# Weight block sums of seven-product sets: two of four made by adding DMAs, and the second weight tile in a slot of its own

## The chip, the cores and the metric

The kernel runs on one core of a Trainium2 chip. The metric is the device time of one execution in microseconds, as a median of several runs.

The core has TensorE (PE: matmuls, and PEld its weight loads), VectorE (DVE), ScalarE (ACT), GpSimd (POOL) and SyncE (SP), which issues most of the DMAs. Each engine carries out its own instructions strictly in the order in which they stand in the program, and waits on semaphores for the others.

## The reference

Two layers of a streaming encoder work on 512 tokens of 1024 channels. Each layer has a feed-forward network (FFN), a mixer of three branches, and a second FFN. The change lies in the FFNs alone:

```python
def swiglu(h, w_gate, w_up, w_down):
    return (jax.nn.silu(h @ w_gate) * (h @ w_up)) @ w_down
    ...
    h = modulate(rms_norm(x, norm_gain[l, 0]), mod[:, 0], mod[:, 1])
    x = x + 0.5 * mod[:, 2][:, None, :] * swiglu(h, ffn_w_gate[l, 0], ffn_w_up[l, 0], ffn_w_down[l, 0])
```

The hidden width is 2816, which is 22 blocks of 128 columns. All inputs are float32.

## The kernel before, in words

**Number format.** TensorE multiplies a rounded format (fp32r). To keep float32 accuracy every operand is split in two: a high half, made by a cast on ScalarE, and a low half, the rest, made by a subtraction on VectorE (`split_to`, L416 to L418). A product is then three matmuls: high by high, high by low, low by high.

**An FFN** goes through the 22 blocks in three parts of 6, 8 and 8 blocks. In each part the gate and up products are made, silu of the one is multiplied with the other, and the result goes through w_down (`k_outer`, L421 on), which adds to the residual x. The blocks of the first part are made directly (all six in the very first FFN, four of six in the others). All other blocks are made in pairs.

**A pair of blocks** is made by a seven-product scheme of block matrices (Winograd's form of Strassen's method): `seven`, L541. It is called once for w_gate (a gate set) and once for w_up (an up set). The weights of the two blocks, each 1024 x 128, form a 2 x 2 grid: A11 and A12 are the first and second half of the first block's rows, A21 and A22 those of the second block. The tokens h form a grid B11 to B22 too. Seven products of half size take the place of eight. Their left sides are A11, A12, A22 and the sums S1 = A21 + A22, S2 = S1 - A11, S3 = A11 - A21, S4 = A12 - S2; their right sides are B11, B21, B22 and the sums T1 to T4, which the class `Blocks` makes once per FFN.

A set does the following. SP loads the two weight tiles of 512 KB ("raw", two buffers, L547). The first tile is split, and A22 too. VectorE makes the four sums (L556 to L559) into two tiles of the "v2" slots, one with S1 and S2, one with S3 and S4. Both are split into tiles of the "ptb" slots. These are two buffers, so the split of a set's S1 and S2 waits until the set before has finished its products with S1 and S2. Then come the products, each of 12 matmuls of 256 columns (4 blocks of rows by 3): A11, A12, S2, S1, S3, S4, A22. Between them ScalarE copies partial results out of PSUM into a tile c, and VectorE adds to it (L573, L582, L583). After an up set, VectorE multiplies with the silu of the gate set (`act`, L624) and splits the result.

**How often.** The second and the third part of each of the four FFNs are a run of eight sets (gate and up in turn). The first part of three FFNs has a lone pair of sets. That makes 8 x 8 + 3 x 2 = 70 sets.

**The order of the work.** Python writes the instructions in the order of the code; small pieces of side work (`later`, `poll`) are put between matmuls by due times. The framework then fixes, when the program is built, in what order each engine's instructions stand, and which buffer each tile gets. SP's queue is also in order: a load that waits for its buffer holds up the loads behind it. MOD_RATE is 0 in the runs of sets, so that the loads of w_ada, which feed the modulation, stand in w_down's stages.

Of the kernel before, what the change touches and what calls it, by code (L numbers as in the profile page):

```python
# [40 lines left out]
def encoder_kernel(tc, xT, c, w_ada, b_ada, gains, w_gate, w_up, w_down, w_qkv, w_f, w_ubg,  # L41
# [443 lines left out]
    def minus(o, a, b):  # L485
        nc.vector.tensor_tensor(o, a, b, op=ALU.subtract)  # L486

    class Blocks:
# [28 lines left out]

        def t1_t3(self, m):
            b1, b2 = self.full[m], self.full[m + 2]
            minus(b1[:, :, FIRST], b1[:, :, SECOND], b1[:, :, FIRST])  # L520
            minus(b1[:, :, SECOND], b2[:, :, SECOND], b1[:, :, SECOND])

        def t2_t4(self, m):
            b1, b2 = self.full[m], self.full[m + 2]
            minus(b2[:, :, SECOND], b2[:, :, SECOND], b1[:, :, FIRST])
            minus(b2[:, :, FIRST], b2[:, :, FIRST], b2[:, :, SECOND])

        def split(self, q):
            self.parts[q] = blk("b"), blk("b")
# [10 lines left out]

    def seven(srcs, blocks, bank):  # L541

        raws = []
        for src in srcs:
            side_work()
            raw = st([P, KD, P], F32, "raw", NRAW)
            last["dma"] = nc.sync.dma_start(raw, src).ins  # L547
            raws.append(raw)
        tens = lambda o, a, b, op: nc.vector.tensor_tensor(o, a, b, op=op)
        a11, a12, a21, a22 = raws[0][:, :4], raws[0][:, 4:], raws[1][:, :4], raws[1][:, 4:]  # L550
        ah, al = duo((KD, P), "w", NARROW)
        split_to(ah, al, raws[0])
# [25 lines left out]
        nc.scalar.copy(c[:, 2], w)  # L578
        go(x, "S3", "T3", False)
        nc.scalar.copy(c[:, 3], x)  # L580
# [15 lines left out]
    class Ffn:  # L596
# [19 lines left out]
        def act(self, n, pg, pu, sg=None):  # L616
            if sg is None:
                sg = apply([pg], AF.Silu)
            pr = t2(T)
            parts = pu if isinstance(pu, list) else [pu]  # L620
            m = T // len(parts)
            for i, p in enumerate(parts):
                cols = slice(i * m, (i + 1) * m)
                nc.vector.tensor_tensor(pr[:, cols], p, sg[:, cols], op=ALU.mult)  # L624
            a = blk("b")
            split_to(a[:, 0, :], a[:, 1, :], pr)
            return a

        def run(self, nxt):
# [4 lines left out]
            for part, (f0, nf) in enumerate(parts):  # L634
# [41 lines left out]
                if not opening:  # L676
                    blocks.finish()
                while n < nf:
                    both = [apply(p, AF.Silu)
                            for p in seven([w_gate[l, s, f0 + n + i] for i in range(2)], blocks, acc)]  # L680
                    ups = seven([w_up[l, s, f0 + n + i] for i in range(2)], blocks, mmt)
                    for i, sg in enumerate(both):
                        acts.append(self.act(n + i, None, ups[i], sg))
                    n += 2
                MOD_RATE[0] = 1.2
                for c0 in (0, T):
# [644 lines left out]
```

## Time and profile before

| what | value |
|---|---|
| time, median of 3 runs | 2368.86 us (2366.21 to 2369.56) |
| the profiled execution's own time | 2370.22 us |
| its span in the profile | 2368.4 us |
| granted TensorE clock | 1.00 |
| bytes moved by DMA | 325.18 MB |

The page gives for each engine its busy time and its share of the span. The rows of groups read: line, engine, operation, output and inputs, count, then busy time and the mean of one, then the idle time of the engine ahead of them and what ended it. Busy time of TensorE is modelled for the ends of matmuls, so the starts of rows tell its pace better than their lengths; the same holds for VectorE and ScalarE, where an instruction's end overlaps the start of the next.

### The profile page before, as it was taken

To read this page: it belongs to the slowest core of one execution; us is meant where nothing else is said; L and a number is where in the kernel's file an instruction comes from. 1 tells how busy PE (TensorE), PEld (TensorE's weight loads), DVE (VectorE), ACT (ScalarE), POOL (GpSimd) and SP (SyncE) were. 2 spreads that over 40 slices of the span, in tenths; PEclk is the share of its full clock that TensorE was granted. 3 is DMA by queue.
4 is the path that set the end of the run, shared out by engine and by line. 5 is a ranking of instruction groups with operands and counts; after the bars stand their busy time and mean duration, and the time that the engine had idled before them with its cause. 6 is when DMAs were issued, how large, how long until landed. Compare 5 with 4: busy or idle time off the path is not lost.

```text
span 2368.4 us, 37435 instructions
## 1 busy us (share of the span) xinstructions
PE 2335.2 (99%) x14322; PEld 2075.8 (88%) x14322; DVE 1770.8 (75%) x3147; ACT 1197.2 (51%) x2097; POOL 326.4 (14%) x433
## 2 busy tenths in 40 slices
PE   7999999999999999999999999999999999999999
PEld 5898998878888898989999989888788888999898
DVE  8887866787686577878687878677866855878583
ACT  5353555676632353635553536456765324636262
POOL 3000011244411100000100000112543211000000
PEclk9999999999999999999999999999999999999999
DMA  8535342333355524353415353533333654143233
GB/s 292 182 107 187 101 167 88 105 99 110 122 199 202 188 71 161 116 187 99 152 63 178 101 185 107 187 107 99 99 122 106 221 199 167 63 142 108 98 100 107
DMA packets 117976, 325.18 MB, mean 137 GB/s; under 512 B 11650, under 2 KB 13826, under 8 KB 117796
## 3 DMA queue, kind: packets, MB, share of 16 engines
q1 hardware_dynamic: 115106, 314.38, 39.9%
q0 software_dynamic: 2688, 8.39, 1.2%
q8 instruction: 113, 1.85, 0.3%
q14 instruction: 67, 0.55, 0.1%
q10 hardware_dynamic: 2, 0.00, 0.0%
HBM read 312.16 MB, written 6.38 MB: 134 GB/s over the span
## 4 chain that ended last, share of the span: by engine, by line
PE 85%; DVE 9%; ACT 3%; DMA 2%; issue 2%; SPq 0%; ACTq 0%; DVEq 0%; POOL 0%; POOLq 0%
PE acc L140 16%; PE acc L142 16%; PE acc L141 16%; PE mm L151 4%; PE mm L149 4%; PE mm L150 4%; PE acc L149 4%; PE acc L151 4%; PE acc L150 4%; PE mm L140 3%; PE mm L142 3%; PE mm L141 3%; PE mm L1020 1%; DVE w L418 1%; DVE v L486 1%
## 5 line engine op out<-in xcount | busy, mean ns | idle before, releaser
L312 DVE TENSOR_TENSOR w<-raw,w 128x1024 fp32r<-128x1024 f32 x247 | 313.2, 1271 | 161.6 <-ACT w L310 161.3
L310 ACT CAST w<-raw 128x1024 fp32r<-128x1024 f32 (+1 forms) x255 | 264.3, 1040 | 273.4 <-PE acc L142 187.5
L140 PE MATMUL acc<-b,w 128*128 128x512 f32 (+1 forms) x960 | 359.8, 375 | 0.0
L141 PE MATMUL acc<-b,w 128*128 128x512 f32 (+1 forms) x960 | 356.3, 371 | 0.0
L142 PE MATMUL acc<-b,w 128*128 128x512 f32 (+1 forms) x960 | 356.1, 371 | 0.0
L142 PEld LDWEIGHTS acc<-b,w 128*128 128x128 f32 x960 | 180.4, 188 | 31.6
L140 PEld LDWEIGHTS acc<-b,w 128*128 128x128 f32 x960 | 180.3, 188 | 30.3
L141 PEld LDWEIGHTS acc<-b,w 128*128 128x128 f32 x960 | 180.6, 188 | 29.8
L417 ACT CAST ptb<-v 128x1024 fp32r<-128x1024 f32 x140 | 146.6, 1050 | 100.8 <-DVE v L486 62.0
L418 DVE TENSOR_TENSOR ptb<-v,ptb 128x1024 fp32r<-128x1024 f32 x140 | 170.7, 1222 | 33.2 <-ACT ptb L417 32.7
L140 PE MATMUL acc<-hhi,w 128*128 128x512 f32 x480 | 191.9, 401 | 2.4 <-ACT hhi L747 1.7
L142 PE MATMUL acc<-hhi,w 128*128 128x512 f32 x480 | 188.8, 393 | 2.6 <-DVE w L312 2.6
L141 PE MATMUL acc<-hlo,w 128*128 128x512 f32 x480 | 188.7, 393 | 0.5 <-DVE hlo L750 0.5
L417 ACT CAST w<-raw 128x1024 fp32r<-128x1024 f32 (+1 forms) x140 | 116.5, 832 | 122.1 <-PE acc L142 56.2
L418 DVE TENSOR_TENSOR w<-raw,w 128x1024 fp32r<-128x1024 f32 (+1 forms) x140 | 133.1, 950 | 13.0 <-ACT w L417 13.0
L140 PE MATMUL acc<-w,hhi 128*128 128x512 f32 x336 | 138.7, 414 | 0.9 <-ACT t L849 0.9
L142 PE MATMUL acc<-w,hlo 128*128 128x512 f32 x336 | 131.9, 392 | 0.0
L141 PE MATMUL acc<-w,hhi 128*128 128x512 f32 x336 | 131.6, 392 | 0.0
L227 DVE CUSTOM_DVE_ANT_0 v<-v,b,badac 128x1024 f32<-128x1024 f32 x87 | 116.8, 1352 | 10.1 <-DMA v<-in_w_ada_dram 10.1
L149 PE MATMUL acc<-b,ptb 128*128 128x256 f32 x420 | 118.3, 282 | 0.0
L150 PE MATMUL acc<-b,ptb 128*128 128x256 f32 x420 | 117.8, 280 | 0.0
L151 PE MATMUL acc<-b,ptb 128*128 128x256 f32 x420 | 117.7, 280 | 0.0
(312 smaller groups left out, 6583.7 us busy)
## 6 DMA issues: line engine op xcount, KB each, us to landing
raw<-in_w_down_dram SPq DMA_DIRECT2D x88, 512.0 KB, 4.1
v<-in_w_ada_dram SPq DMA_DIRECT2D x87, 512.0 KB, 5.1
raw<-in_w_up_dram SPq DMA_DIRECT2D x82, 512.0 KB, 3.6
raw<-in_w_gate_dram SPq DMA_DIRECT2D x79, 512.0 KB, 3.6
b<-in_w_ada_dram SPq DMA_DIRECT2D x57, 512.0 KB, 4.7
raw<-in_w_ubg_dram SPq DMA_DIRECT2D x56, 512.0 KB, 3.6
raw<-in_w_qkv_dram SPq DMA_DIRECT2D x42, 512.0 KB, 3.7
raw<-in_w_branch_dram SPq DMA_DIRECT2D x24, 512.0 KB, 3.7
```

What stands on the lines that cost most here:

```text
L140: mm(o, lh, rh, start=start, stop=False)
L141: mm(o, lh, rl, start=False, stop=False)
L142: mm(o, ll, rh, start=False, stop=stop)
L149: mm(o, lh, rh, start=start and k == 0, stop=False, skip_group_check=True)
L150: mm(o, lh, rl, start=False, stop=False, skip_group_check=True)
L151: mm(o, ll, rh, start=False, stop=k == 3, skip_group_check=True)
L227: dot = nc.vector.tensor_tensor_reduce(out=raw, in0=raw, in1=silc[0], scale=1.0, scalar=badac[:, l, j, d:d + 1], op0=ALU.mult, op1=ALU.add ...
L310: nc.scalar.copy(hi, raw)
L312: lo_eng.tensor_tensor(lo, raw, hi.bitcast(F32), op=ALU.subtract)
L417: nc.scalar.copy(hi, src)
L418: nc.vector.tensor_tensor(lo, src, hi.bitcast(F32), op=ALU.subtract)
L486: nc.vector.tensor_tensor(o, a, b, op=ALU.subtract)
```

## The change

In `seven`, S3's first half and S1's second step now come from DMAs that add. The second block's weights go into a tile of the "pta" slot, which has one buffer and which attention uses in the mixer. SP first loads A11 into the place of S3 (a plain load of 256 KB, in addition to the two tiles). Then GpSimd issues two DMAs of 256 KB that add what they read to what stands in the tile: A21 onto A11, which gives A11 + A21, and A22 onto A21, which gives A21 + A22 in place of A21. VectorE makes the two other sums, as additions. The sums are additions because the second block column takes the opposite sign: T1 to T4 are turned, silu of the second block is taken at scale -1, and its product is multiplied by -1 (two-operation instructions take the place of one-operation ones there). As the second tile is no longer in "raw", that slot's two buffers hold the first tiles of two sets, and "v2" gets two tiles per set in place of three.

```diff
         def t1_t3(self, m):
             b1, b2 = self.full[m], self.full[m + 2]
-            minus(b1[:, :, FIRST], b1[:, :, SECOND], b1[:, :, FIRST])
+            minus(b1[:, :, FIRST], b1[:, :, FIRST], b1[:, :, SECOND])
             minus(b1[:, :, SECOND], b2[:, :, SECOND], b1[:, :, SECOND])
 
         def t2_t4(self, m):
             b1, b2 = self.full[m], self.full[m + 2]
-            minus(b2[:, :, SECOND], b2[:, :, SECOND], b1[:, :, FIRST])
-            minus(b2[:, :, FIRST], b2[:, :, FIRST], b2[:, :, SECOND])
+            for half, other in ((SECOND, b1[:, :, FIRST]), (FIRST, b2[:, :, SECOND])):
+                t = b2[:, :, half]
+                nc.vector.scalar_tensor_tensor(t, other, -1.0, t, op0=ALU.mult, op1=ALU.subtract)
...
     def seven(srcs, blocks, bank):
 
-        raws = []
-        for src in srcs:
-            side_work()
-            raw = st([P, KD, P], F32, "raw", NRAW)
-            last["dma"] = nc.sync.dma_start(raw, src).ins
-            raws.append(raw)
+        top, low = srcs
+        s34 = st([P, 2, 4, P], F32, "v2", 4)
+        side_work()
+        nc.sync.dma_start(s34[:, 0], top[:, :4])
+        r0 = st([P, KD, P], F32, "raw", NRAW)
+        last["dma"] = nc.sync.dma_start(r0, top).ins
+        side_work()
+        r1 = st([P, 2, 4, P], F32, "pta", 1)
+        last["dma"] = nc.sync.dma_start(r1.rearrange("p a k c -> p (a k) c"), low).ins
+        nc.gpsimd.dma_start(s34[:, 0], low[:, :4], accum_op=ALU.add)
+        nc.gpsimd.dma_start(r1[:, 0], low[:, 4:], accum_op=ALU.add)
...
-        split_to(bh, bl, a22)
-        s12, s34 = st([P, 2, 4, P], F32, "v2", 4), st([P, 2, 4, P], F32, "v2", 4)
-        tens(s12[:, 0], a21, a22, ALU.add)
-        minus(s34[:, 0], a11, a21)
-        minus(s12[:, 1], s12[:, 0], a11)
-        minus(s34[:, 1], a12, s12[:, 1])
+        split_to(bh, bl, r1[:, 1])
+        tens(r1[:, 1], r1[:, 0], r0[:, :4], ALU.add)
+        tens(s34[:, 1], r1[:, 1], r0[:, 4:], ALU.add)
         pair12, pair34 = duo((2, 4, P), "ptb"), duo((2, 4, P), "ptb")
-        split_to(*pair12, s12)
+        split_to(*pair12, r1)
         split_to(*pair34, s34)
...
-                nc.vector.tensor_tensor(pr[:, cols], p, sg[:, cols], op=ALU.mult)
+                if sign == 1.0:
+                    nc.vector.tensor_tensor(pr[:, cols], p, sg[:, cols], op=ALU.mult)
+                else:
+                    nc.vector.scalar_tensor_tensor(pr[:, cols], p, sign, sg[:, cols], op0=ALU.mult, op1=ALU.mult)
...
-                    both = [apply(p, AF.Silu)
-                            for p in seven([w_gate[l, s, f0 + n + i] for i in range(2)], blocks, acc)]
+                    gates = seven([w_gate[l, s, f0 + n + i] for i in range(2)], blocks, acc)
+                    both = [apply(p, AF.Silu, scale=sign) for p, sign in zip(gates, (1.0, -1.0))]
```

The fixed order of the engines changes with it. The rows below are from the first run of eight sets, in the first FFN; the other runs read alike. Line numbers of the kernel after lie 2 to 5 higher in this part.

First place: VectorE between the first up set and the gate set behind it (the third set). Before, it reads as follows; `ptb_206` is the low half of the third set's S1 and S2, `mm_191` the last result of the up set ahead of it, `t2` and `b` belong to the activation, and `w_219` is the first tile of the fourth set.

```order
L418 TENSOR_TENSOR ptb_206_1224<-v2_203_1217,ptb_206_1224 128x1024
L549 TENSOR_TENSOR v2_194_1104<-v2_194_1104 128x256
L549 TENSOR_TENSOR v2_194_1104<-mm_193_1103,v2_194_1104 128x256
L624 TENSOR_TENSOR t2_195_1196<-v2_194_1104,t1_177_1070 128x512
L624 TENSOR_TENSOR t2_197_1201<-v2_194_1104,t1_178_1072 128x256
L418 TENSOR_TENSOR ptb_209_1227<-v2_204_1218,ptb_209_1227 128x1024
L418 TENSOR_TENSOR b_196_1198<-t2_195_1196,b_196_1198 128x512
L624 TENSOR_TENSOR t2_197_1201<-mm_191_1101,t1_178_1072 128x256
L418 TENSOR_TENSOR w_219_1337<-raw_217_1333,w_219_1337 128x1024
L418 TENSOR_TENSOR b_198_1204<-t2_197_1201,b_198_1204 128x512
```

After, the same place reads as follows; `ptb_203` is now the low half of S1 and S2, `pta_199` the tile of the second weights, `mm_189` the last result of the up set, `w_217` the first tile of the fourth set.

```order
L555 TENSOR_TENSOR v2_192_1104<-v2_192_1104 128x256
L555 TENSOR_TENSOR v2_192_1104<-mm_191_1103,v2_192_1104 128x256
L627 TENSOR_TENSOR t2_193_1196<-v2_192_1104,t1_176_1070 128x512
L629 SCALAR_TENSOR_TENSOR t2_195_1201<-v2_192_1104,t1_177_1072 128x256
L629 SCALAR_TENSOR_TENSOR t2_195_1201<-mm_189_1101,t1_177_1072 128x256
L555 TENSOR_TENSOR pta_199_1211<-pta_199_1211,raw_198_1209 128x512
L418 TENSOR_TENSOR b_194_1198<-t2_193_1196,b_194_1198 128x512
L555 TENSOR_TENSOR v2_197_1207<-pta_199_1211,raw_198_1209 128x512
L418 TENSOR_TENSOR b_196_1204<-t2_195_1201,b_196_1204 128x512
L418 TENSOR_TENSOR w_217_1341<-raw_215_1335,w_217_1341 128x1024
L418 TENSOR_TENSOR ptb_203_1224<-pta_199_1211,ptb_203_1224 128x1024
```

The low half of S1 and S2 moved from ahead of the up set's last sums and its activation to behind all of them, and behind the first tile of the set after.

Second place: VectorE in the third set, ahead of the fourth. Before, with `acc_213` the result that S4's product of the third set ends, and `ptb_224` the fourth set's S1 and S2:

```order
L486 TENSOR_TENSOR v2_221_1343<-v2_221_1343,raw_217_1333 128x512
L486 TENSOR_TENSOR v2_222_1344<-raw_217_1333,v2_221_1343 128x512
L418 TENSOR_TENSOR ptb_224_1350<-v2_221_1343,ptb_224_1350 128x1024
L549 TENSOR_TENSOR v2_214_1236<-acc_213_1235,v2_214_1236 128x256
L549 TENSOR_TENSOR v2_214_1236<-v2_214_1236 128x256
L418 TENSOR_TENSOR ptb_227_1353<-v2_222_1344,ptb_227_1353 128x1024
```

After, with `acc_210` that result, and `ptb_220` the fourth set's S1 and S2:

```order
L418 TENSOR_TENSOR w_218_1344<-pta_216_1337,w_218_1344 128x512
L555 TENSOR_TENSOR v2_211_1236<-v2_211_1236 128x256
L555 TENSOR_TENSOR v2_211_1236<-acc_210_1235,v2_211_1236 128x256
L555 TENSOR_TENSOR pta_216_1337<-pta_216_1337,raw_215_1335 128x512
L555 TENSOR_TENSOR v2_214_1333<-pta_216_1337,raw_215_1335 128x512
L418 TENSOR_TENSOR ptb_220_1350<-pta_216_1337,ptb_220_1350 128x1024
```

The fourth set's sum and the low half of its S1 and S2 moved behind the sum that takes S4's result of the third set. ScalarE's cast for that split likewise stands behind the silus of the third set.

Third place: TensorE after the third set's product with A12 (`acc_209`). Before, all twelve matmuls of each product stood together in the order A11, A12, S2, S1, S3, S4, A22, set by set. Now, with `mm_225` and `mm_226` the fourth set's products with A11 and A12, and `acc_208` and `acc_210` the third set's with S2 and S1:

```order
L149 MATMUL mm_225_1359<-hhi_111,w_217_1341 128x256
L149 MATMUL acc_210_1235<-b_110_620,ptb_203_1224 128x256
L150 MATMUL acc_210_1235<-b_111_621,ptb_203_1224 128x256
L150 MATMUL mm_225_1359<-hlo_112,w_217_1341 128x256
L149 MATMUL mm_226_1360<-hhi_111,w_217_1341 128x256
L150 MATMUL mm_226_1360<-hlo_112,w_217_1341 128x256
L151 MATMUL mm_225_1359<-hhi_111,w_217_1341 128x256
L149 MATMUL acc_208_1233<-b_123_683,ptb_203_1224 128x256
L150 MATMUL acc_208_1233<-b_124_684,ptb_203_1224 128x256
```

Some matmuls of the fourth set's first two products moved in among the third set's; from the first with S1 to the end of S4, 59 matmuls stand where 48 belong to the third set. On SP the load of a set's "pta" tile stands behind the load of the first tile of the set after, and waits for the low half of S1 and S2 of the set before. GpSimd's queue holds the two adding DMAs of each set, and nothing else in these stretches.

More of the change, by code (lines that the diff above doesn't have):

```diff
@@ L541, in seven @@
     def seven(srcs, blocks, bank):
-        raws = []
-        for src in srcs:
-            side_work()
-            raw = st([P, KD, P], F32, "raw", NRAW)
-            last["dma"] = nc.sync.dma_start(raw, src).ins
-            raws.append(raw)
+        top, low = srcs
[9 more added lines that the diff above has]
+        nc.gpsimd.dma_start(r1[:, 0], low[:, 4:], accum_op=ALU.add)
         tens = lambda o, a, b, op: nc.vector.tensor_tensor(o, a, b, op=op)
-        a11, a12, a21, a22 = raws[0][:, :4], raws[0][:, 4:], raws[1][:, :4], raws[1][:, 4:]
         ah, al = duo((KD, P), "w", NARROW)
-        split_to(ah, al, raws[0])
+        split_to(ah, al, r0)
         bh, bl = duo((4, P), "w", NARROW)
-        split_to(bh, bl, a22)
-        s12, s34 = st([P, 2, 4, P], F32, "v2", 4), st([P, 2, 4, P], F32, "v2", 4)
-        tens(s12[:, 0], a21, a22, ALU.add)
-        minus(s34[:, 0], a11, a21)
-        minus(s12[:, 1], s12[:, 0], a11)
-        minus(s34[:, 1], a12, s12[:, 1])
+        split_to(bh, bl, r1[:, 1])
+        tens(r1[:, 1], r1[:, 0], r0[:, :4], ALU.add)
+        tens(s34[:, 1], r1[:, 1], r0[:, 4:], ALU.add)
         pair12, pair34 = duo((2, 4, P), "ptb"), duo((2, 4, P), "ptb")
-        split_to(*pair12, s12)
+        split_to(*pair12, r1)
         split_to(*pair34, s34)
@@ L614, in unit, with act @@
                        k == 0, k == KD - 1)
-        def act(self, n, pg, pu, sg=None):
+        def act(self, n, pg, pu, sg=None, sign=1.0):
             if sg is None:
@@ L678, in run @@
                 while n < nf:
-                    both = [apply(p, AF.Silu)
-                            for p in seven([w_gate[l, s, f0 + n + i] for i in range(2)], blocks, acc)]
+                    gates = seven([w_gate[l, s, f0 + n + i] for i in range(2)], blocks, acc)
+                    both = [apply(p, AF.Silu, scale=sign) for p, sign in zip(gates, (1.0, -1.0))]
                     ups = seven([w_up[l, s, f0 + n + i] for i in range(2)], blocks, mmt)
                     for i, sg in enumerate(both):
-                        acts.append(self.act(n + i, None, ups[i], sg))
+                        acts.append(self.act(n + i, None, ups[i], sg, (1.0, -1.0)[i]))
                     n += 2
```

## The prediction

> **What bounds the kernel now.** I read the page first: the busy shares, the clock and the chain.
>
> ```profile
> PE 2335.2 (99%) x14322; PEld 2075.8 (88%) x14322; DVE 1770.8 (75%) x3147; ACT 1197.2 (51%) x2097; POOL 326.4 (14%) x433
> PEclk9999999999999999999999999999999999999999
> PE 85%; DVE 9%; ACT 3%; DMA 2%; issue 2%; SPq 0%; ACTq 0%; DVEq 0%; POOL 0%; POOLq 0%
> ```
>
> TensorE is never idle for long, always at full clock, and makes 85% of the chain. So VectorE time that is saved gains only where TensorE waits. How much that is in the sets of seven products, the waits of PE tell (time in total, times, longest):
>
> ```profile
> PE acc L149 <- ACT v L580: 4.5, 8, 0.7
> PE mm L149 <- ACT v L580: 1.0, 2, 0.7
> ```
>
> That is 5.5 us in the whole execution: the most that the edited code can give back. Then the timeline: two sets that follow each other, by their first product, and the windows (PE, PEld, DVE, ACT, POOL busy; clock, DMA share, GB/s).
>
> ```profile
> 123.62 0.28 PE L149 MATMUL acc<-hhi,w 128*128 128x256 f32 x1
> 133.51 0.28 PE L149 MATMUL mm<-hhi,w 128*128 128x256 f32 x1
> ```
>
> ```profile
> 134.00:144.00 10.00, 10.00 (x88) 10.00 (x86) 8.55 (x14) 6.07 (x12) 0.00 (x0) 1.00 0.38 112
> 144.00:154.00 10.00, 10.00 (x87) 10.00 (x86) 9.53 (x15) 6.51 (x12) 0.00 (x0) 1.00 0.27 94
> 200.00:210.00 10.00, 10.00 (x59) 8.77 (x58) 9.93 (x19) 3.52 (x5) 0.00 (x0) 1.00 0.93 327
> ```
>
> One set takes 9.89 us for 84 matmuls, 0.118 us each, 12 to a product (1.41 us). VectorE is 86 to 95% busy beside it: close, yet in time. How far ahead it is, its timeline shows:
>
> ```profile
> 137.86 0.68 DVE L486 TENSOR_TENSOR v<-raw,raw 128x512 f32<-128x512 f32 x1
> 138.46 0.69 DVE L486 TENSOR_TENSOR v<-v,raw 128x512 f32<-128x512 f32 x1
> 139.18 0.69 DVE L486 TENSOR_TENSOR v<-raw,v 128x512 f32<-128x512 f32 x1
> 140.72 1.23 DVE L418 TENSOR_TENSOR ptb<-v,ptb 128x1024 fp32r<-128x1024 f32 x1 [0.85 <-ACT ptb L417]
> 141.86 0.42 DVE L549 TENSOR_TENSOR v<-v 128x256 f32<-128x256 f32 x1
> 142.20 0.42 DVE L549 TENSOR_TENSOR v<-mm,v 128x256 f32<-128x256 f32 x1
> 142.65 1.03 DVE L624 TENSOR_TENSOR t<-v,t 128x512 f32<-128x512 f32 x2
> 143.60 1.22 DVE L418 TENSOR_TENSOR ptb<-v,ptb 128x1024 fp32r<-128x1024 f32 x1
> 144.73 0.68 DVE L418 TENSOR_TENSOR b<-t,b 128x512 fp32r<-128x512 f32 x1
> 145.34 0.41 DVE L624 TENSOR_TENSOR t<-mm,t 128x256 f32<-128x256 f32 x1
> 145.67 1.21 DVE L418 TENSOR_TENSOR w<-raw,w 128x1024 fp32r<-128x1024 f32 x1
> 146.80 0.68 DVE L418 TENSOR_TENSOR b<-t,b 128x512 fp32r<-128x512 f32 x1
> ```
>
> The low half of S1 and S2 for the third set ("lo12" below) is done at 141.95. That set starts at 133.51 + 9.89 = 143.4, and reaches S2 two products later, at 146.2: 4.3 us of lead. Starts also give the pace of VectorE: 0.60 us for 512 columns, 1.14 for 1024, 0.34 for 256; a dependent reader waits for the full 0.69, 1.22, 0.42.
>
> **What the change removes.** Two sums per set:
>
> ```profile
> L549 DVE TENSOR_TENSOR v<-raw x70: 679/692/695, 114.4 to 2306.1; 128x512 f32<-128x512 f32 x70
> L486 DVE TENSOR_TENSOR v<-raw,raw x70: 679/684/690, 116.2 to 2306.7; 128x512 f32<-128x512 f32 x70
> ```
>
> 70 x (0.692 + 0.684) = 96 us of VectorE, 1.38 us per set, none of it on TensorE's path beyond the 5.5 us above. The turned signs (in T1 to T4, in silu and in the second activation) replace an operation by one of the same shape: I cost them at nothing; a tenth of a microsecond each on VectorE would be hidden by the 1.38 us.
>
> **What it adds and moves.** Per set one load of 256 KB (SP) and two adding DMAs of 256 KB (GpSimd): 70 x 768 KB = 55 MB. A set's 1.05 MB become 1.84 MB, 184 GB/s at the old pace; w_down's stage moved 327 GB/s (200 to 210 us above), so bandwidth alone isn't the limit. The second weight tile has one buffer ("pta"), where raw had two. Its next load is issued when the last reader, lo12, is done; then come the load, the adding DMA, a sum, the cast and the next lo12. The rows for this loop:
>
> ```profile
> raw<-in_w_gate_dram SPq DMA_DIRECT2D x79, 512.0 KB, 3.6
> x_dram<-xv POOLq DMA_DIRECT2D x8, 512.0 KB, 3.1
> strip<-in_rel_dram SPq DMA_DIRECT2D x16, 256.0 KB, 2.6
> v<-in_w_ada_dram SPq DMA_DIRECT2D x87, 512.0 KB, 5.1
> L417 ACT CAST ptb<-v 128x1024 fp32r<-128x1024 f32 x140 | 146.6, 1050 | 100.8 <-DVE v L486 62.0
> ```
>
> ```profile
> 133.30 0.63 ACT L592 ACTIVATE t<-v 128x512 f32<-128x512 f32 x1
> 133.84 0.36 ACT L592 ACTIVATE t<-acc 128x256 f32<-128x256 f32 x1
> 134.10 0.41 ACT L592 ACTIVATE t<-v 128x256 f32<-128x256 f32 x1
> 134.41 1.04 ACT L417 CAST w<-raw 128x1024 fp32r<-128x1024 f32 x1
> ```
>
> No row shows an adding DMA. Its lower bound is a plain one of its size, 2.6 us; its upper, 512 KB in a busy queue, 5.1. I take 3.9: as if its 256 KB moved twice (3.6), and 0.3 for GpSimd's issue. [...] A wake costs about 0.05, rounded up from this cast, which ends at 140.69, and the subtraction at 140.72 above:
>
> ```profile
> 139.64 1.05 ACT L417 CAST ptb<-v 128x1024 fp32r<-128x1024 f32 x1
> ```
>
> Load and add then take 3.6 + 3.9 + 0.2 for wakes = 7.7 us from one lo12.
>
> The order matters more. Before, lo12 stands ahead of the second activation's pieces; now it is queued behind them, behind products of the set before. Call t the end of lo12.
>
> From a gate set to its up set (the second place of VectorE's order): after t TensorE runs 59 matmuls to the end of S4 (57 in the first pair, 64 in the third and fourth, where pieces of the next set are put between): 6.95 us, + 0.16 for the last result. VectorE's sum of c takes 0.42; ScalarE's silus ahead of the cast 0.54 + 0.31 (their starts above); the cast 1.05; lo12 1.22; five wakes 0.25. Sum 10.9 (10.65 in the first pair, 11.5 in the last two). The weight sum runs beside the silus and is hidden if the tile is there by 7.8: it is, at 7.7.
>
> From an up set to the next gate set (the first place): 48 matmuls to the end of S4, 5.65 + 0.16; the sum of c 0.42; then in VectorE's queue product 0.6, product 0.34, weight sum 0.6, low half 0.6, product 0.34, weight sum 0.6, the next set's first tile 1.14, low half 0.6, lo12 1.22 = 6.04; three wakes: 12.4. The weight sum would start at 7.3, the tile comes at 7.7: + 0.4 = 12.8.
>
> A run of eight sets (two in each of four FFNs): its first lo12 now stands behind the residual of w_down's last product, 0.7 + 0.6 + 1.14 + 1.22 + 0.16 = 3.8 after the run begins; then 10.65 + 10.9 + 2 x 11.5 = 44.55 and 3 x 12.8 = 38.4; after the last lo12 sixty matmuls, 7.1. Sum 93.9 us, against 8 x 9.89 = 79.1: 14.8 more, x 8 runs = 118. The three lone pairs have their lo12 early: nothing. The 5.5 us of old waits are within these stretches: 112.5 more than now. The profiled execution took 2370.2 us (span 2368.4), 1.4 above the median of 2368.9, so the forecast for a median is 2481 us.
>
> The bounds: an adding DMA at 2.6 us takes off only the 0.4 x 24 = 10 (2471), since the order binds. At 5.1 the tile comes at 8.9: the three stretches lose 1.2 more each, the four 1.35, 1.1, 0.5 and 0.5: 7 x 8 = 57 more (2538). Loads that land 0.6 later under the added traffic: 0.6 x 7 x 8 = 34 (2572). On the low side, each step of the loop 0.4 shorter takes 0.4 x 7 x 8 = 22, and a run's start that hides takes 8: 2451.
>
> **The rivals.** *A slow adding DMA.* Over 5.7 us it leaves my range (0.6 above 5.1 costs 34). At 7 us it alone sets the loop: 3.6 + 7 + 0.2 + 0.7 + 1.05 + 1.22 + 0.2 = 14 us, 7 x 14 + 11 = 109 per run, 30 more than now, 8 runs: 240, less the 5.5: 2603. [...] Against it: GpSimd's issues lie between 561 and 751 ns beside a busy VectorE.
>
> ```profile
> L1176 POOL DMA_DIRECT2D x_dram<-xv x8: 561/572/751, 343.1 to 1542.6; - x8
> ```
>
> [...]
>
> *VectorE was the hidden limit, and TensorE gains* (the other side): with 1.38 us less per set, the late copies (L580) come in time and the 5.5 us go: 2363. It decides for this if the step from lo12 to lo12 is at most 9.9 us. For it: VectorE at 95% in every second set. Against it: the queue orders above give 10.7 to 12.8 whatever the DMA does.
>
> *The sums were off the path and the loop hides as well*: the single buffer's lateness stays within the 4.3 us of lead: 2369.
>
> *Half of it hides*: TensorE's next-set pieces, put ahead of S2, fill more than I count, and half of the 112 stays: 2425. For it: they are 24 matmuls, 2.8 us; against it: I have counted them as done before the wait ends.
>
> **How the numbers follow.** Forecast 2481 us, range 2451 to 2572 from the bounds: 0.80. Slow adding DMA 0.09, half hidden 0.05, unchanged 0.03, gain 0.03. About 0.2% (4.7 us) is what a measurement here tells from no change. So faster 0.03, same 0.03, slower 0.94.
>
> **What would show it.** In the new profile: PE busy falls, with waits of L149 to L151 on VectorE's L418 of some 110 us in all, in pairs of sets that take about 23.5 us instead of 19.8; VectorE some 90 us less busy; the adding DMA's landing near 3.9 us; the pta load issued just after lo12. Wrong if sets still take 9.9 us, if TensorE waits instead on sums that wait for the adding DMA, or if the loss lies in w_down or the mixer.

## The result, and the profile after

The kernel after takes 2584.94 us (median of 4 runs, 2581.53 to 2588.61) against 2368.04 of the kernel before: ratio 1.0917, 95% interval 1.0898 to 1.0935. That is 217 us slower; 112.5 were forecast. The profiled execution took 2586.32 us, its span is 2584.5.

First the page: busy shares, clock, the chain.

```profile
PE 2424.0 (94%) x14322; PEld 2139.8 (83%) x14322; DVE 1696.7 (66%) x3007; ACT 1193.0 (46%) x2097; POOL 445.7 (17%) x573
PEclk9999989999999999998999999999999999998989
PE 59%; DMA 19%; DVE 12%; issue 5%; ACT 4%; POOL 0%; POOLq 0%; ACTq 0%; SPq 0%; DVEq 0%
```

And the row of the core, with its mean granted clock:

```profile
core 0: 2584.5 us, clock 0.969
```

DMAs, 2% of the chain before, are 19% now. TensorE was 99% busy and is now 94%. But its busy time *rose*, from 2335.2 to 2424.0 us, with the same 14322 matmuls, and the mean granted clock fell from 1.00 to 0.969. So there are two losses: waits, and slower matmuls. The waits of TensorE (total, times, longest):

```profile
PE mm L149 <- ACT ptb L417: 88.6, 32, 4.3
PE mm L151 <- DVE ptb L418: 14.0, 21, 0.8
PE mm L151 <- DVE w L418: 13.3, 21, 1.0
PE acc L149 <- ACT v L582: 10.0, 8, 2.8
PE acc L149 <- ACT ptb L417: 4.7, 12, 0.9
```

These are 130.6 us where 5.5 stood before: 125 more. 107.3 of them are waits for the split of S1 and S2 (tile `ptb`), where the forecast put them, and ScalarE's cast (L417) ends most of these, VectorE's low half (L418) the rest. That 125 lies near the 112.5 of the forecast is partly luck, since slow matmuls fill time that would have been waits too. The rest of the loss is the 88.8 us of longer busy time. What it looks like, in TensorE's timeline of the second set (an up set):

```profile
137.20 0.28 PE L151 MATMUL mm<-hhi,w 128*128 128x256 f32 x1
139.71 0.39 PE L149 MATMUL mm<-b,ptb 128*128 128x256 f32 x1 [2.23 <-ACT ptb L417]
139.93 0.28 PE L150 MATMUL mm<-b,ptb 128*128 128x256 f32 x1
140.97 0.58 PE L151 MATMUL mm<-b,ptb 128*128 128x256 f32 x1 [0.76 <-DVE ptb L418]
141.35 0.42 PE L149 MATMUL mm<-b,ptb 128*128 128x256 f32 x1
141.56 0.42 PE L150 MATMUL mm<-b,ptb 128*128 128x256 f32 x1
...
144.46 0.28 PE L149 MATMUL mm<-b,ptb 128*128 128x256 f32 x1
144.57 0.28 PE L150 MATMUL mm<-b,ptb 128*128 128x256 f32 x1
```

A pause of 2.5 us, a second short one, and then starts 0.21 us apart instead of 0.113, until 144.2. The windows over the same place (PE, PEld, DVE, ACT, POOL busy; clock, DMA share, GB/s) give the reason in the clock column:

```profile
138.00:140.00 2.00, 0.29 (x2) 0.29 (x2) 1.54 (x3) 1.39 (x3) 0.00 (x0) 1.00 0.00 0
140.00:142.00 2.00, 1.24 (x7) 1.04 (x7) 2.00 (x2) 2.00 (x3) 0.00 (x0) 0.73 0.72 233
142.00:144.00 2.00, 2.00 (x11) 2.00 (x11) 1.60 (x3) 0.09 (x1) 0.01 (x1) 0.50 1.02 369
144.00:146.00 2.00, 2.00 (x18) 2.00 (x18) 0.00 (x0) 1.04 (x3) 0.86 (x1) 0.92 0.31 66
```

Behind the pause the granted clock is 0.50 for about 3.4 us. The trace's clock has 35 such falls in the sets, one in each up set: 23 of 3.4 us and 12 of 6.8 us.

The loop that makes the pause shows in VectorE's timeline, from the low half of S1 and S2 of the first set ("lo12") to that of the third:

```profile
127.85 1.22 DVE L418 TENSOR_TENSOR ptb<-pta,ptb 128x1024 fp32r<-128x1024 f32 x1
...
137.84 0.69 DVE L555 TENSOR_TENSOR pta<-pta,raw 128x512 f32<-128x512 f32 x1 [2.63 <-DMA pta<-in_w_up_dram]
...
139.69 1.23 DVE L418 TENSOR_TENSOR ptb<-pta,ptb 128x1024 fp32r<-128x1024 f32 x1 [0.43 <-ACT ptb L417]
...
148.06 0.42 DVE L555 TENSOR_TENSOR v<-mm,v 128x256 f32<-128x256 f32 x1 [0.53 <-PE mm L151]
...
150.76 0.69 DVE L555 TENSOR_TENSOR pta<-pta,raw 128x512 f32<-128x512 f32 x1 [0.88 <-DMA pta<-in_w_gate_dram]
...
154.31 1.22 DVE L418 TENSOR_TENSOR ptb<-pta,ptb 128x1024 fp32r<-128x1024 f32 x1
```

lo12 ends at 129.07 (start plus length), 140.92 and 155.53: steps of 11.85 and 14.61 us, where 10.65 and 12.8 were forecast and a set needs 9.89. In both steps the weight sum waits for the adding DMA, 8.77 and 9.84 us after the lo12 before it; the forecast had 7.7. Over the whole execution these waits of VectorE are (total, times, longest):

```profile
DVE pta L555 <- DMA pta<-in_w_up_dram: 94.3, 35, 4.2
DVE pta L555 <- DMA pta<-in_w_gate_dram: 14.4, 18, 1.3
```

So the weight sum waits for the adding DMA in every step to an up set (32 in the runs of eight, 3 in the lone pairs) and in 18 of the 24 steps to a gate set. In the runs it starts 9.05 and 9.53 us after lo12 (means of the two kinds of step).

In SP's and GpSimd's timelines, the two loads go out just behind lo12, and the adding DMAs 4.6 and 5.2 us later:

```profile
129.10 0.33 SPq L552 DMA_DIRECT2D pta<-in_w_up_dram  x1
...
140.94 0.33 SPq L552 DMA_DIRECT2D pta<-in_w_gate_dram  x1
```

```profile
133.67 0.86 POOL L554 DMA_DIRECT2D pta<-in_w_up_dram  x1 [15.49 <-DMA pta<-in_w_up_dram]
...
146.11 0.86 POOL L554 DMA_DIRECT2D pta<-in_w_gate_dram  x1 [1.25 <-DMA pta<-in_w_gate_dram]
```

Not all of the 4.6 us is the load. ScalarE's cast of the same tile starts as soon as the load is there, 4.1 us after its issue; GpSimd starts 0.48 us after ScalarE:

```profile
133.19 0.62 ACT L417 CAST w<-pta 128x512 fp32r<-128x512 f32 x1 [1.10 <-DMA pta<-in_w_up_dram]
```

From the first to the last matmul of L149 to L151 in TensorE's timeline, a run of eight sets takes 102.7 to 106.5 us (before: 78.8 to 80.1), a lone pair 23.4 to 23.9 (before: 19.7). Over the eight runs and three pairs that is 910.0 against 693.9 us: 216.1 more, and the spans differ by 216.1. The whole loss lies in the sets.

### The profile page after: what moved, and what is told of

Read it like the earlier page. It is cut to its first block, busy times and chain, and to the rows that moved or that the text cites. A ratio compares the mean times of both kernels' runs of the same rounds, so it can differ in the third digit from the quotient of the medians.

```text
span 2584.5 us, 37809 instructions
## 1 busy us (share of the span) xinstructions
PE 2424.0 (94%) x14322; PEld 2139.8 (83%) x14322; DVE 1696.7 (66%) x3007; ACT 1193.0 (46%) x2097; POOL 445.7 (17%) x573
## 4 chain that ended last, share of the span: by engine, by line
PE 59%; DMA 19%; DVE 12%; issue 5%; ACT 4%; POOL 0%; POOLq 0%; ACTq 0%; SPq 0%; DVEq 0%
PE acc L142 14%; PE acc L140 14%; PE acc L141 14%; DMA pta<-in_w_up_dram 11%; DMA pta<-in_w_gate_dram 7%; PE mm L140 3%; PE mm L141 3%; PE mm L142 3%; DVE ptb L418 3%; PE mm L151 2%; DVE pta L555 2%; PE mm L149 2%; PE mm L150 2%; ACT ptb L417 2%; DVE v L227 1%
## 5 line engine op out<-in xcount | busy, mean ns | idle before, releaser
L310 ACT CAST w<-raw 128x1024 fp32r<-128x1024 f32 (+1 forms) x255 | 264.4, 1041 | 273.1 <-PE acc L142 166.4
L149 PE MATMUL mm<-b,ptb 128*128 128x256 f32 x420 | 147.9, 353 | 88.6 <-ACT ptb L417 88.6
L149 PEld LDWEIGHTS mm<-b,ptb 128*128 128x128 f32 x420 | 107.9, 257 | 95.0 <-ACT ptb L417 95.0
L418 DVE TENSOR_TENSOR w<-pta,w 128x512 fp32r<-128x512 f32 x70 | 48.5, 693 | 187.3 <-ACT w L417 187.3
L151 PE MATMUL mm<-b,ptb 128*128 128x256 f32 x420 | 142.9, 355 | 14.4 <-DVE ptb L418 14.0
L150 PE MATMUL mm<-b,ptb 128*128 128x256 f32 x420 | 143.1, 342 | 0.0
L467 DVE SCALAR_TENSOR_TENSOR xv<-acc,badac,xv 128x512 f32<-128x512 f32 (+1 forms) x112 | 77.4, 691 | 88.6 <-PE acc L142 88.4
L149 PE MATMUL acc<-b,ptb 128*128 128x256 f32 x420 | 118.6, 283 | 4.9 <-ACT ptb L417 4.7
```

The source lines that it names most:

```text
L149: mm(o, lh, rh, start=start and k == 0, stop=False, skip_group_check=True)
L150: mm(o, lh, rl, start=False, stop=False, skip_group_check=True)
L151: mm(o, ll, rh, start=False, stop=k == 3, skip_group_check=True)
L310: nc.scalar.copy(hi, raw)
L418: nc.vector.tensor_tensor(lo, src, hi.bitcast(F32), op=ALU.subtract)
L467: nc.vector.scalar_tensor_tensor(x, acc_j, gate, x, op0=ALU.mult, op1=ALU.add)
```

## The experiments

**Theory**: with one buffer for the weight tile, the set's pace is a loop: lo12, load, adding DMA, weight sum, cast, lo12. It is longer than a set, and the pauses also drop TensorE's clock. **Rivals**: the order of the instructions alone binds (the prediction); adding DMAs cost by themselves; DMA traffic, not the clock, slows the matmuls; the signs cost.

All steps below are read as above, from one lo12's end to the next, in the eight runs of sets: means of 32 steps from a gate to an up set, and of 24 from an up to a gate set.

| kernel | time, us | gate to up | up to gate | clock |
|---|---|---|---|---|
| after | 2584.9 | 12.12 | 14.51 | 0.969 |
| after, order of before | 2569.2 | 12.75 | 13.34 | 0.980 |
| after, load cut in two | 2514.2 | 11.28 | 12.38 | 0.988 |
| after, copies instead of adds | 2505.3 | 10.75 | 13.36 | 0.986 |
| after, sums by VectorE | 2413.2 | 10.05 | 9.93 | 0.999 |

**1. The signs alone.** The kernel before with every sum an addition and the turned signs:

```diff
-        minus(s34[:, 0], a11, a21)
+        tens(s34[:, 0], r0[:, :4], raw1[:, :4], ALU.add)
```

> The kernel before with the turned signs alone: all four weight sums are additions made by VectorE in the tiles of before, T1 to T4 turned, silu of the second block at scale -1, its product at -1; no added DMA, no other slot. Theory (the signs cost nothing): 2367 to 2371 us. Rival (two-operation instructions in T1 to T4 and in the second activation are slower, or the order that comes with them makes TensorE wait): 2380 us or more.

Measured: 2367.32 us, ratio 1.0001 (0.9992 to 1.0010). The signs cost nothing, as forecast: a two-operation product of 256 columns takes 418 ns, the one-operation one of before took 417.

**2. Pauses of known length.** Blocks of 100 matmuls wait for a chain of k VectorE operations on 64 columns:

```diff
+                for _ in range(k):
+                    nc.vector.tensor_scalar(h[:, :64], h[:, :64], 0.5, None, op0=ALU.mult)
+                t = block(100, g)
```

> This kernel leaves the whole encoder out: it runs 70 blocks of 100 matmuls of the sets' shape (128x128 by 128x256), each block waiting on a chain of VectorE operations of growing length behind the block before, so that TensorE pauses for some 1 to 8 us, five times each; no DMA runs beside it. Theory (a pause of some 2 to 4 us drops the granted clock, and the matmuls behind it run at about 0.21 us instead of 0.113 until some 3 us of work are done): behind short pauses the pace is 0.113 us, behind pauses of over 2 to 4 us about 30 of the 100 matmuls take 0.21 us and a block takes about 3 us longer. Rival (the slow matmuls in the changed kernel come from DMA traffic in SBUF): pace 0.113 us in all blocks, whatever the pause.

Rows of TensorE's timeline, one for a block; in brackets its idle time before:

```profile
163.68 12.25 PE L59 MATMUL o<-g,lhs 128*128 128x256 f32 x100 [1.31 <-DVE g L70]
191.71 12.26 PE L59 MATMUL o<-g,lhs 128*128 128x256 f32 x100 [1.76 <-DVE g L70]
205.73 13.75 PE L59 MATMUL o<-g,lhs 128*128 128x256 f32 x100 [1.76 <-DVE g L70]
405.13 13.75 PE L59 MATMUL o<-g,lhs 128*128 128x256 f32 x100 [3.14 <-DVE g L70]
1063.93 13.76 PE L59 MATMUL o<-g,lhs 128*128 128x256 f32 x100 [7.26 <-DVE g L70]
```

No DMA runs here, and still a block behind a long pause takes 1.5 us more (1.3 to 2.7 in all; the theory's 3 was too much), and the run's mean granted clock is 0.889. Up to 1.31 us of idle time none of 10 blocks is slow; at 1.76 us 1 of 5, at 2.22 2 of 5, at 2.68 3 of 5, from 3.14 on all 45. The same pause does it or doesn't, and no run here shows what decides. Pauses of 1.76 to 2.68 us are thus not safe: 6 of the 15 blocks behind them are slow. So a pause alone is enough for slow matmuls, and in the kernel after they stand where its clock reads 0.50: DMA traffic is not needed to explain them.

**3. Copies instead of adds**, with the same order on every engine (the other DMA likewise):

```diff
-        nc.gpsimd.dma_start(r1[:, 0], low[:, 4:], accum_op=ALU.add)
+        nc.gpsimd.dma_start(r1[:, 0], low[:, 4:])
```

> The kernel after with the two GpSimd DMAs of a set as plain copies, no add: this leaves two of the four weight sums out. The order of every engine is the same as after, so only the landing time of these DMAs can change. Theory (the loop through the one buffer, load then adding DMA then sum then cast then low half, sets the pace, and the add costs about 1.4 us over a plain DMA of 256 KB): tile ready 1.4 us earlier, the loop shorter by up to 0.9 us in the steps to an up set and 1.4 us in the steps to a gate set, 32 x 0.9 + 24 x 1.4 = 62 us less, and up to 89 us more where pauses get too short to drop the clock: 2435 to 2525 us. Rival (the order alone binds, as the prediction had it): at most 10 to 20 us less, 2565 to 2575. Rival (an adding DMA costs as much as a plain one): 2585.

Measured: 2505.29 us, ratio 1.0582 (1.0563 to 1.0602): 80 us less than after. The DMA's rows, after and then this kernel (KB each, median us from issue to landing):

```profile
pta<-in_w_up_dram POOLq DMA_DIRECT2D x35, 256.0 KB, 4.3
```

```profile
pta<-in_w_up_dram POOLq DMA_DIRECT2D x35, 256.0 KB, 2.9
```

The add costs 1.4 us of landing time, and GpSimd's issue 0.862 us where a copy's takes 0.536. The steps to an up set fall by 1.37: there the adding DMA sets the pace, and "the order alone binds" falls. The steps to a gate set fall by 1.15, and stay at 13.4. There the weight sum waits for the DMA in 9 of 24 steps, where it did in 18; in the others the order binds, with slow matmuls in it.

**4. The load cut in two**, so that the add can begin when A21's half is there:

```diff
-        last["dma"] = nc.sync.dma_start(r1.rearrange("p a k c -> p (a k) c"), low).ins
+        nc.sync.dma_start(r1[:, 0], low[:, :4])
+        last["dma"] = nc.sync.dma_start(r1[:, 1], low[:, 4:]).ins
```

> The kernel after with the load of the pta tile cut into two of 256 KB, A21 first, so that S1's adding DMA can start when A21's half has landed. Theory (the time from the low half to the finished tile, 8.75 to 10 us, sets the steps): the adding DMA starts 0.7 to 1.2 us earlier, 56 steps, 40 to 65 us less: 2520 to 2545 us. Rival of the prediction (the order alone binds): 2575 to 2590 us.

Measured: 2514.19 us, ratio 1.0619 (1.0603 to 1.0635), 71 us less, a little more than the theory had. Adding stays, and the weight sum starts 0.86 us (steps to an up set) and 0.55 us (to a gate set) earlier. But VectorE's order shifted too: in the steps to a gate set lo12 ends 3.39 us after the weight sum starts, where it was 4.99. So the shorter loop is only a part of the 71 us.

**5. The order of before**, by an edge that holds S4's sum back:

```diff
+            tc.add_manual_dep(held_back[0], lo12.name, mybir.DependencyInfo(
+                mybir.DependencyClass.NoSync, mybir.DependencyReason.DATA), reason="order")
```

> The kernel after, one pta buffer, with an order edge in each run of sets: VectorE's sum that takes S4's result stands behind the low half of the next set's S1 and S2, as before the change. Theory (loop and order both cost; the loop of load, adding DMA, sum, cast and low half takes about 9.8 + 3.1 = 12.9 us at most, 11.85 in the steps to up sets that are bound by it already): the steps to gate sets fall from 14.7 to some 12.9, 24 to 28 of them, 43 to 50 us less, and less clock is lost: 2490 to 2545 us. Rival of the prediction (the order alone binds, the DMAs hide): 2370 to 2400 us. Rival (the order costs nothing, all is the loop): 2575 to 2585 us.

Measured: 2569.15 us, ratio 1.0846 (1.0826 to 1.0866): only 16 us less, and the theory's 40 to 95 were too many. Steps to a gate set fall by 1.2, as it had it, but those to an up set rise by 0.6. With lo12 early in the queue, all steps behind a run's first have means of 12.8 to 13.7 us, and in all 56 the weight sum waits for the adding DMA: that is the loop. The prediction's 2370 to 2400 is out by far.

**6. One buffer, sums by VectorE**: no adding DMA, no added load.

```diff
-        nc.gpsimd.dma_start(r1[:, 0], low[:, 4:], accum_op=ALU.add)
...
+        tens(r1[:, 0], r1[:, 0], r1[:, 1], ALU.add)
```

> The kernel after with the one pta buffer, but all four sums by VectorE: no adding DMA and no added load. The tile is then finished a load and two or three sums after the low half of the set before. Theory (the adding DMA in the loop makes the loss: without it load 3.8 to 4.6, four VectorE steps 2.8, cast 1.05, low half 1.2 are about 9 to 9.6 us, less than the 9.89 us of a set): 2368 to 2430 us. Rival of the prediction (the order that the one buffer brings binds by itself, steps of 10.7 to 12.4 us): 2460 to 2530 us.

Measured: 2413.19 us, ratio 1.0191 (1.0170 to 1.0213). One buffer without the DMAs costs 45 us, with steps of some 10 us, hardly over a set, and a clock of 0.999. The other 172 us come with the DMAs in the loop, and with what they did to the order: here lo12 stands ahead of the activation's low halves and of the next set's first tile, no longer behind them. This run does not part the two; experiment 5 shows that an early lo12 with the DMAs still in the loop gains 16 us.

**7. Another slot for the weight tile**: v2 (four buffers).

```diff
-        r1 = st([P, 2, 4, P], F32, "pta", 1)
+        r1 = st([P, 2, 4, P], F32, "v2", 4)
```

> The kernel after with the second weight tile in a v2 slot (four buffers, three used by a set) in place of pta. The order of the instructions on VectorE and ScalarE stays nearly that of after: the low half of S1 and S2 still stands behind the last sums and the activation of the set before. Theory of the prediction (the order binds, the DMAs add only 0.4 us): waits of TensorE still some 100 us, and the clock still drops: 2500 to 2560 us. Rival (the one buffer binds, since it puts load and adding DMA into the loop): loads start a set earlier, TensorE waits under 30 us, clock near 1.00, 2370 to 2400 us.

Measured: 2573.81 us, ratio 1.0874 (1.0858 to 1.0890). This did not do what it was for. Three tiles of a set and one that comes fill the four buffers, and the first to come free is the weight tile's own: its load still goes out at lo12's end (127.77, lo12 ending at 127.74). The loop is the same (steps of 11.79 and 14.93 us).

**8. Two pta buffers** (t2 with one, for room).

```diff
-        r1 = st([P, 2, 4, P], F32, "pta", 1)
+        r1 = st([P, 2, 4, P], F32, "pta", 2)
...
-        return st([P, cols], F32, "t2", 3)
+        return st([P, cols], F32, "t2", 1)
```

> The kernel after with two buffers for the pta slot; to make room, the slot t2 (the products ahead of an activation's split) has one buffer in place of three. The order that the framework makes is then that of before: the low half of S1 and S2 stands ahead of the last sums of the set before. Theory (the one buffer is the cause of all of it, the loop through load and adding DMA, the late order, the pauses and the clock): TensorE waits under 20 us in the sets, clock 1.00, 2366 to 2385 us, of which up to 10 is the smaller t2. Rival (the adding DMAs and their traffic cost time by themselves, or slow the matmuls): 2400 us or more, with slow matmuls at no pause.

Measured: 2493.57 us, ratio 1.0527 (1.0494 to 1.0559): 91 us less than after, and the order is that of before without any edge. The theory's 2366 to 2385 is out; the time lies on the rival's side. The waits for S1 and S2's split are gone. In their place stand these, of TensorE and of ScalarE:

```profile
PE acc L149 <- ACT v L574: 57.6, 18, 5.8
```

```profile
ACT ptb L417 <- DMA v<-in_w_gate_dram: 94.0, 19, 7.6
```

The other adding DMA, S3's, is late: its A11 load stands last in SP's queue, and its issue behind that for the next set's weight tile on GpSimd's (141.26 behind 140.72). ScalarE's cast waits for it, and the copy that frees PSUM waits behind the cast.

**9. Half of the change, S3's adding DMA**, with the weight tiles in raw as before and S1 by VectorE.

```diff
-        nc.gpsimd.dma_start(r1[:, 0], low[:, 4:], accum_op=ALU.add)
+        tens(r1[:, 0], raw1[:, :4], raw1[:, 4:], ALU.add)
```

> Half of the change: S3's first half by the added load and one adding DMA, the turned signs, but S1 by VectorE, with the second weight tile in raw as before and S1 and S2 in v2. The adding DMA is then in no loop through a single buffer. Theory (the adding DMA costs nothing where there is time for it): 2364 to 2374 us, VectorE busy 48 us less than before. Rival (adding DMAs slow VectorE, the loads or TensorE by themselves): over 2390 us.

Measured: 2374.09 us, ratio 1.0029 (1.0017 to 1.0042). That is the edge of the theory's range, and 6 us more than before. The 70 adding DMAs land in 4.1 us and cost little: they start early enough. What remains is one wait, once per run of sets (5.5 us stood there before):

```profile
PE mm L149 <- ACT v L575: 13.7, 8, 3.5
```

VectorE is 38 us less busy (1732.6; 48 were expected), and nothing is won by it.

**10. S1's adding DMA alone**, in three places. With one and with two pta buffers:

```diff
-        nc.sync.dma_start(s34[:, 0], top[:, :4])
...
-        nc.gpsimd.dma_start(s34[:, 0], low[:, :4], accum_op=ALU.add)
+        tens(s34[:, 0], r0[:, :4], r1[:, 0], ALU.add)
```

> As the kernel with only S1 by an adding DMA, but with the one pta buffer of the change. Theory (the loop load, adding DMA, sum, cast, low half binds): steps of 11.5 to 14 us from one low half to the next, 2530 to 2580 us, against 2364 to 2385 with two buffers. Rival (the S3 chain, the A11 load and the other adding DMA, makes the loss): 2370 to 2400 us.

> Only S1 by an adding DMA (no added load of A11, S3 by VectorE), and two buffers for the pta slot (t2 with one). Theory (the one buffer's loop is the cause, and the adding DMA costs nothing once it stands outside a loop): no waits on the splits of S1 and S2, 2364 to 2385 us. Rival (an adding DMA into the weight tile costs time by itself): over 2400 us.

Measured: 2585.59 us (1.0895 to 1.0932) with one buffer: the loss is that of after without S3's DMAs, so the weight tile's loop is enough for it. That the two times agree is partly luck: the steps are 13.4 and 13.3 us here, 12.12 and 14.51 in the kernel after. With two: 2516.74 us (1.0608 to 1.0644), and the theory missed again. The reason is in GpSimd's waits:

```profile
POOL pta L554 <- DVE v L552: 807.7, 36, 61.7
```

The add overwrites A21, so it must wait for VectorE's S3 sum, which still reads A21 (with one buffer too). With two, in five of a run's seven steps that sum ends 0.6 to 2.7 us after lo12, and the steps have means of 9.6 to 10.4 us; in two it ends 5.9 us after, and they have 13.7 and 13.9. Then in a v2 tile of its own, with the weight tiles in raw:

```diff
+        nc.sync.dma_start(r1[:, 0], low[:, :4])
+        nc.gpsimd.dma_start(r1[:, 0], low[:, 4:], accum_op=ALU.add)
```

> Only S1 by an adding DMA, and that in a v2 tile of its own (SP loads A21 there, GpSimd's DMA adds A22); both weight tiles in raw as before, S3 by VectorE. So the adding DMA neither overwrites a tile that others read nor stands between a weight tile's release and its next load. Theory (an adding DMA costs nothing outside such a loop): 2364 to 2385 us. Rival (the time from its tile's slot coming free to the sum is again over a set's 9.89 us): steps of 11 us and more, over 2420 us.

Measured: 2503.81 us, ratio 1.0573 (1.0551 to 1.0595): the rival's side. The load of A21 waits in SP's queue until the lo12 before it has freed the slot (138.28, lo12 ending at 138.25). Again load and add follow each other within the step, and the steps are mostly 11 to 13 us. No kernel here has S1's adding DMA outside such a loop; that it would cost nothing there is shown for S3's alone.

**11. The pauses filled with work.** 24 matmuls more, in the gate sets and then in the up sets, into a PSUM tile that S1 overwrites. This is the edit for the up sets; for the gate sets it has `acc` in place of `mmt`:

```diff
+        if bank is mmt:
+            for rep in range(2):
+                go(w, "A11", "B11", True)
         go(x, "S2", "T2", False)
```

> The kernel after with 24 matmuls more in each gate set, ahead of S2 and into a PSUM tile that S1 overwrites afterwards, so that TensorE works through most of its pause: 35 x 24 x 0.113 = 95 us of added work, no other value changed. Theory (the pause drops the clock, and the drop costs some 80 us): the matmuls of S2 that had a mean of 0.19 us fall towards 0.115, clock 0.99 or more; the pauses of some 85 us are filled: 2585 + 95 - 85 - 60 to 80 = 2515 to 2535 us. Rival (the matmuls behind the pause are slow through DMA traffic or operand reads): they stay at 0.19 us, 2585 to 2680 us.

> The kernel after with 24 matmuls more in each up set (where the kernel after has its longest pauses, ahead of S2), into a PSUM tile that S1 overwrites afterwards: 35 x 24 x 0.113 = 95 us of work without a result. Theory (pauses drop the clock; the steps are set by the loop of load and adding DMA, and the slow matmuls only lengthen the steps in which the order binds): S2's matmuls go back to 0.115 to 0.12 us, clock 0.99, the steps stay at 12 to 13.5 us: 2545 to 2585 us, no slower than after in spite of 95 us more work. Rival (the slow matmuls are no matter of the pause): they stay near 0.19 us, 2620 us or more.

Measured: 2581.78 us (one run) in the gate sets and 2632.70 us (two runs) in the up sets; clock 0.987 and 0.980. In the first, busy time rose by 38 us (2462.1) though 95 us of work were added: some 57 us of slow matmuls are gone. But the time did not fall, though the theory had it so; steps are 12.8 us throughout. The second missed by 48 us: behind the filled pause S2's matmuls start 0.114 us apart again, but the pauses moved to other products. In both the order changed too. In the kernel after the clock falls in the up sets, so the first did not fill the pauses that mattered, and its better clock goes with the changed order. The second shows that the clock holds behind a filled pause; neither shows what the clock alone is worth.

## Why the prediction was wrong

The side was right, and so was the place: TensorE waits at S2 for a lo12 that comes late through the one buffer; the pta load goes out just behind lo12; the removed VectorE work (74 us measured, 96 forecast) and the signs are worth nothing. What makes lo12 late was wrong, and with it the size, in these steps.

**"The order matters more"; an adding DMA at 2.6 us "takes off only the 0.4 x 24 = 10".** With copies that land in 2.9 us, 80 went. The prediction took load and add as hidden behind the order, with 0.1 us to spare in the steps to an up set. The term that failed is the time from lo12 to the finished tile: put at 7.7 us, it was 9.05 and 9.53 in the mean. GpSimd's issue came 4.44 and 5.14 us after lo12, where 3.6 and a wake were put: the load landed in 3.8 and 4.6 us (medians), and the wake, put at about 0.05, is near 0.5 there. From the issue to the weight sum it took 4.61 and 4.39 instead of 3.9. The 3.9 was the author's estimate: 256 KB added cost as much as 512 KB copied (3.6), and 0.3 us go to GpSimd's issue. No run shows either term: the adding DMAs landed in 4.2 to 4.6 us (medians), copies of the same bytes from the same queue in 2.9 to 3.3, and the issue takes 0.86. So TensorE did wait "on sums that wait for the adding DMA", which the prediction named as what would make it wrong. To an up set, 9.05 us and 3.07 from the weight sum to lo12's end are the measured 12.12, one microsecond over the forecast mean of 11.14, in 32 steps. To a gate set, 9.53 and 4.99 are 14.5 us instead of 12.8, in 24 steps. That is 31 and 41 us of the 104 that were missed.

**The pace of 0.118 us, taken behind pauses too.** The step to a gate set was worked out from 48 matmuls in 5.65 us. Behind the pause they run at half clock for 3.4 us or twice that, a loss that the prediction put at nothing: the sum that takes S4's result starts at 148.06, 7.14 after lo12, where 5.65 + 0.16 were put. This alone would have made the step long. Without its wait for the DMA (0.60 us in the mean) the weight sum would start 8.93 us after lo12, and the step would take some 13.9 us. But the tile came later still in 18 of the 24 steps, so there half clock and DMA overlap, and the DMA ends last. The end of a run (8.4 us instead of 7.1) has half clock too.

Three smaller things in the prediction were off without much effect. In the step to a gate set it put the activation's third product behind the weight sum; VectorE's order has it ahead. By that order the weight sum would start at 7.65 us and the step be 12.5 instead of 12.8: an error the other way. And of the eight issues of GpSimd "beside a busy VectorE", the one of 751 ns ran beside an idle one. The added traffic, 1.84 MB in 9.89 us, is 186 GB/s, not 184.

**"The three lone pairs have their lo12 early: nothing."** Their second set runs through the same loop (12.25 to 12.84 us): 3.9 us each, 12 in all.

The sum, by the means: 4.44 to the first lo12, 4 x 12.12, 3 x 14.51, 8.42 behind the last: 104.9 us a run, 11 more than the forecast 93.9. Eight times 11 and 12 for the pairs are 100, and the miss was 104. The upper end of the range, 2572, did allow for a tile at 8.9 + 0.6 = 9.5 us; what it had no room for were the lone pairs and the half clock.

What the two causes are worth apart is settled only in part. Without DMAs in the loop (experiment 6) both pauses and half clock go, and 172 us with them, but lo12's place changes too. With the order of before and the DMAs in the loop (experiment 5) 201 us of loss stay. By the mean clock, half clock is 80 us of TensorE's time (0.031 x 2584.5); where the DMA ends last, full clock would only have made longer waits. What is left for it alone is some 18 us, an estimate: 1.3 at each of eight runs' ends, and up to 1.2 (8.93 less 7.7) in the 6 steps to a gate set without a wait for the DMA. That is worked out and not shown: no run took away the clock's fall and nothing else.

Of the rivals, "VectorE was the hidden limit" got no support: with S3's sum off it, the time was 1.0029 of before. The slow adding DMA did not come at its threshold (5.7 us); but its idea, that the DMA and not the order sets the loop, was the nearer one.

## What to carry to other kernels

Before moving a sum from an engine to an adding DMA, write down the loop through its buffer, from release to release, with every DMA in it: two that follow each other took 9.05 and 9.53 us here in the mean, nearly a whole set, while the sum that they replaced took 0.69. Set this against what the order allows, since the later of the two decides. More buffers help only if the tile that comes free is not the one still waited for; look in the queue's order for what the load stands behind. And price a pause of TensorE not by its length alone: here the matmuls could be slow behind pauses of 1.76 us and more, 1.3 to 2.7 us on top (experiment 2), and in the kernel after the granted clock then read 0.50 for 3.4 or 6.8 us. Then ask whether something else ends later still, as the DMA did here.

## What the runs showed of the hardware

- An adding DMA of 256 KB landed in 4.2 to 4.6 us in the kernel after, a copy of the same bytes in 2.9 to 3.3 from the same queue (medians); GpSimd's issue takes 0.86 us instead of 0.54. The landing time is 1.3 to 1.5 times that of a copy, and no run shows the rate of the transfer by itself.
- GpSimd's DMA started about 0.5 us after what it waited for: 0.48 after ScalarE's start on the same load in the kernel after, and 0.51 to 0.58 (means by step) after VectorE's S3 sum in the kernels of experiment 10 with one and two pta buffers.
- In experiment 2 (mean granted clock 0.889) 1 of 5 blocks of matmuls was slow behind a pause of 1.76 us, and all 45 were behind 3.14 us and more; a slow block took 1.3 to 2.7 us longer, whatever the pause from 3 to 8 us.
